# The sine product of the q and k rotations on VectorE instead of GpSimd

## The chip, the cores and the metric

The kernel runs on one core of a Trainium2 chip. The core has five engines with a queue each: TensorE (PE in the profile, its weight loads PEld), VectorE (DVE), ScalarE (ACT), GpSimd (POOL) and SyncE (SP). Each engine works through a queue of its own in the program's order, and semaphores hold an instruction until what it needs is there. The metric is the device time of one execution in microseconds (us); less is better.

## The reference, cut to what matters

Two networks follow one another, of two layers each, on 512 tokens of width 1024. One mixing layer of the first network is a differential attention of 8 heads; both mixing layers of the second contain, among other attentions, a dilated attention with three branches of four heads. In these, queries and keys are rotated by their position before the scores:

```python
def rotate_half(t):
    half = t.shape[-1] // 2
    return jnp.concatenate([-t[..., half:], t[..., :half]], axis=-1)

def diff_attention_mixer(x, w_qkv, ...):
    ...
    q = (q * cos + rotate_half(q) * sin) * (DIFF_HEAD_DIM ** -0.5)
    k = k * cos + rotate_half(k) * sin
    ...
    scores = jnp.einsum('bhmqd,bhmkd->bhmqk', q[:, :, :, s0:s1], k[:, :, :, :s1], ...)
    p = jax.nn.softmax(jnp.where(mask, scores, NEG_INF), axis=-1)
    attn = p[:, :, 0] - lam * p[:, :, 1]

def _mixing(x, w_in, ...):
    ...
    q = br(_rope(flat(q), pos))
    k = br(_rope(flat(k), pos))
    o_dil = _dilated_attention([q[:, :, i] for i in range(N_BR)], ...)
```

## The kernel before, in words

All products run in an exact split form: a float32 matrix is split into a high part (`split`, L217, a copy on ScalarE) and a low part (L218, a subtraction on VectorE), and `mm3` (L266 to L268) adds three matmuls. Weights arrive in 1024-column halves and are split the same way; they appear as `wpart` and `wmore`.

A rotation (`rope2`, L1185) works on one 128x512 tile of q or k that TensorE has just finished in PSUM: one column group of two heads, or of one head with two maps. Four 32-row pieces are moved into a scratch tile `sh`, two by ScalarE (L1191) and two by VectorE (L1192). The scratch is multiplied by the sines (L1193), the PSUM tile by the cosines (L1194, VectorE), the two are added (L1195, VectorE), and the sum is split into its parts (L217, L218; tiles `dr` in the differential attention, `qd` in the mixing layers of the second network). There are 40 rotations: 16 in the differential attention (4 at its start, 12 in its heads), 12 in each of the two later mixing layers.

In the differential attention the heads run as one pipeline (`diff_head`, `pipelined`). Of each of four query tiles i = 0..3 of a head: scores on TensorE (L872, with the mask L874), two maxima (L876, VectorE), two exponentials with their sums (L878, ScalarE), a reciprocal, a small product and the difference of the two maps (L884, L885, L886, VectorE), transposes on TensorE (L1232) copied out by ScalarE (L1234), and the product with the values (L894). The q and k columns of the next heads (`diff_qk`, 16 steps of three matmuls a head, two rotations a head) are woven in between, and so are the splits of the weights that a later head needs (`done`, `pump`). TensorE's order is the program's own (`manual_schedule`); the queues of VectorE, ScalarE and GpSimd are ordered by a scheduler from the dependences, so a change of one instruction can move others. A half of a weight part may be overwritten only when TensorE has finished the step that still reads it.

Of a head's two rotations, the one that falls near the scores of tile 2 is called the early one below, the one near tile 3 the late one.

Of the kernel before, what the change touches and what calls it, by code (L numbers as in the profile page):

```python
# [129 lines left out]
class _Net:  # L130
# [1054 lines left out]
    def rope2(self, ps, parts, classes, scale=1.0):  # L1185


        nc = self.nc
        sh, t = self.grab(), self.grab()
        for o in (0, 64):  # L1190
            nc.scalar.activation(sh[o:o + 32], ps[o + 32:o + 64], AF.Copy, scale=scale)  # L1191
            nc.vector.tensor_scalar(sh[o + 32:o + 64], ps[o:o + 32], scale, None, op0=ALU.mult)  # L1192
        nc.gpsimd.tensor_mul(sh, sh, self.c("sin"))  # L1193
        nc.vector.scalar_tensor_tensor(t, ps, scale, self.c("cos"), op0=ALU.mult, op1=ALU.mult)  # L1194
        nc.vector.tensor_add(t, t, sh)  # L1195
        if classes:
            parts = [x.rearrange("p (r j) -> p j r", r=4) for x in parts]
            self.split(*parts, t.rearrange("p (j r) -> p j r", r=4))
        else:
            self.split(*parts, t)  # L1200
        self.drop(sh, t)
# [1110 lines left out]
```

## Time and profile before

| | |
|---|---|
| median of 3 runs | 2736.17 us (2734.69 to 2741.09) |
| profiled execution | 2736.06 us, span 2734.3 us |
| TensorE matmul busy | 2610.4 us (95%) |
| VectorE busy | 1663.5 us (61%) |
| ScalarE busy | 1313.9 us (48%) |
| GpSimd busy | 452.2 us (17%) |

The span is the time from the first to the last instruction of the profiled execution; what is left to its own time lies outside. Shares are means over stages with different limits. A busy TensorE is a TensorE with a matmul in flight, and a few matmul records are missing from the trace.

### The profile page before, as it was taken

The numbers are of one execution on the slowest core, as the hardware profiler recorded it, in microseconds if no ns is written. First come the engines' busy times: TensorE is split into PE (matmuls) and PEld (weight loads), VectorE is DVE, ScalarE is ACT, GpSimd is POOL, SyncE is SP. The second block draws the span as 40 slices with busy tenths as digits, with TensorE's granted clock in tenths as the row PEclk, the third lists the DMA queues.
The fourth block names the chain that finished last, engine by engine and source line by source line (L and its number), as shares of the span: only waits on it lengthen the run. The fifth ranks groups of instructions, "written<-read, shape, count | busy, mean of one in ns | idle before, by whom it ended". The sixth has DMA issues, their size and how long they took to land. (4 is left out here: it accounts for less than half of the span.)

```text
span 2734.3 us, 41301 instructions
## 1 busy us (share of the span) xinstructions
PE 2610.4 (95%) x14504; PEld 2194.2 (80%) x14508; DVE 1663.5 (61%) x2633; ACT 1313.9 (48%) x2074; POOL 452.2 (17%) x430
## 2 busy tenths in 40 slices
PE   8999999999999999999999979999899999899996
PEld 6768888887668888898887768888788877788884
DVE  7786333376866333366445586669774455847887
ACT  5644222255644222245464436558654554246784
POOL 2324000010114000002021121211120211212112
PEclk9999999999999999999999989999999999899998
DMA  6114232313104323224202059979532030479995
GB/s 228 52 47 170 93 101 93 108 64 108 62 32 143 104 87 107 96 90 155 87 28 108 19 190 290 307 216 364 179 129 98 32 118 19 152 242 296 346 356 183
DMA packets 94490, 389.23 MB, mean 142 GB/s; under 512 B 14880, under 2 KB 16672, under 8 KB 77984
## 3 DMA queue, kind: packets, MB, share of 16 engines
q1 hardware_dynamic: 76592, 329.14, 34.1%
q0 software_dynamic: 14624, 51.52, 6.9%
q10 hardware_dynamic: 3024, 5.56, 0.6%
q8 instruction: 118, 1.93, 0.3%
q14 instruction: 132, 1.08, 0.1%
HBM read 351.31 MB, written 34.87 MB: 141 GB/s over the span
## 5 line engine op out<-in xcount | busy, mean ns | idle before, releaser
L218 DVE TENSOR_TENSOR wpart<-raw,wpart 128x1024 fp32r<-128x1024 f32 (+3 forms) x393 | 532.5, 1384 | 289.8 <-ACT wpart L217 280.4
L217 ACT ACTIVATE wpart<-raw 128x1024 fp32r<-128x1024 f32 (+3 forms) x393 | 446.4, 1169 | 364.7 <-PE mm L267 182.4
L266 PE MATMUL mm<-xT,wpart 128*128 128x512 f32 (+1 forms) x1136 | 438.2, 386 | 22.0 <-ACT wpart L217 9.0
L267 PE MATMUL mm<-xT,wpart 128*128 128x512 f32 (+1 forms) x1136 | 425.4, 375 | 1.9 <-DVE xT L218 1.9
L268 PE MATMUL mm<-xT,wpart 128*128 128x512 f32 (+1 forms) x1136 | 425.5, 375 | 0.5 <-DVE wpart L218 0.5
L266 PEld LDWEIGHTS mm<-xT,wpart 128*128 128x128 f32 x1136 | 216.6, 191 | 59.8 <-ACT wpart L217 9.0
L268 PEld LDWEIGHTS mm<-xT,wpart 128*128 128x128 f32 x1136 | 215.9, 190 | 39.4 <-DVE wpart L218 1.0
L267 PEld LDWEIGHTS mm<-xT,wpart 128*128 128x128 f32 x1136 | 216.4, 190 | 37.1 <-DVE xT L218 2.9
L266 PE MATMUL mm<-wpart,xT 128*128 128x256 f32 (+2 forms) x672 | 241.1, 359 | 0.0
L268 PE MATMUL mm<-wpart,xT 128*128 128x256 f32 (+2 forms) x672 | 227.0, 339 | 0.4 <-DVE xT L218 0.3
L267 PE MATMUL mm<-wpart,xT 128*128 128x256 f32 (+2 forms) x672 | 226.1, 336 | 0.0
L352 POOL TENSOR_TENSOR sm<-sm,mhalf 128x4 f32<-128x4 f32 (+2 forms) x66 | 61.0, 925 | 978.0 <-DVE sm L365 728.1
L267 PE MATMUL mm<-wpart,gT 128*128 128x256 f32 (+1 forms) x544 | 186.9, 344 | 2.2 <-DVE wpart L218 2.2
L268 PE MATMUL mm<-wpart,gT 128*128 128x256 f32 (+1 forms) x544 | 184.1, 338 | 0.0
L266 PE MATMUL mm<-wpart,gT 128*128 128x256 f32 (+1 forms) x544 | 183.9, 338 | 0.0
L571 DVE TENSOR_TENSOR silu<-silu,mm 128x512 f32<-128x512 f32 x44 | 30.2, 686 | 194.5 <-PE mm L268 194.5
L266 PEld LDWEIGHTS mm<-wpart,xT 128*128 128x128 f32 x672 | 127.8, 190 | 18.0 <-issue 5.2
L218 DVE TENSOR_TENSOR xT<-raw,xT 128x1024 fp32r<-128x1024 f32 x108 | 130.0, 1221 | 15.9 <-ACT xT L217 15.3
L268 PEld LDWEIGHTS mm<-wpart,xT 128*128 128x128 f32 x672 | 127.6, 190 | 14.1 <-DVE xT L939 1.0
L267 PEld LDWEIGHTS mm<-wpart,xT 128*128 128x128 f32 x672 | 128.0, 190 | 9.6 <-issue 1.2
L266 PE MATMUL mm<-xT,hT 128*128 128x512 f32 x272 | 112.9, 415 | 5.7 <-DVE rt L2125 4.5
L267 PEld LDWEIGHTS mm<-wpart,gT 128*128 128x128 f32 x544 | 104.2, 191 | 17.0 <-DVE wpart L218 4.3
(590 smaller groups left out, 5632.8 us busy)
## 6 DMA issues: line engine op xcount, KB each, us to landing
raw<-in_w_dram SPq DMA_DIRECT2D x324, 512.0 KB, 7.4
raw<-in_gu_dram SPq DMA_DIRECT2D x40, 1024.0 KB, 4.7
raw<-in_w_in_dram SPq DMA_DIRECT2D x30, 1024.0 KB, 4.8
raw<-in_down_dram SPq DMA_DIRECT2D x16, 1024.0 KB, 5.1
raw<-in_o_qk_dram SPq DMA_DIRECT2D x8, 1024.0 KB, 4.7
raw<-in_w_out_dram SPq DMA_DIRECT2D x8, 1024.0 KB, 5.2
raw<-in_e_in_dram SPq DMA_DIRECT2D x7, 1024.0 KB, 7.3
raw<-in_down_dram SPq DMA_DIRECT2D x8, 768.0 KB, 4.3
```

The source lines that it names most:

```text
L217: ins = self.nc.scalar.activation(hi, x, AF.Copy)
L218: self.last_lo = (eng or self.nc.vector).tensor_sub(lo, x, hi)
L266: mm(out, lhsT=ls[0], rhs=rs[0], start=start, stop=False)
L267: mm(out, lhsT=ls[0], rhs=rs[1], start=False, stop=False)
L268: mm(out, lhsT=ls[1], rhs=rs[0], start=False, stop=stop)
L352: self.last_rsqrt = self.nc.gpsimd.tensor_tensor(v, v, self.half[:, :n], op=ALU.pow)
L571: nc.vector.tensor_mul(s, s, ps[2 * j + 1])
```

## The change

One line: the multiplication of the scratch tile by the sines is issued on VectorE instead of GpSimd. Operands, sizes and results are the same.

```diff
@@ rope2
         for o in (0, 64):
             nc.scalar.activation(sh[o:o + 32], ps[o + 32:o + 64], AF.Copy, scale=scale)
             nc.vector.tensor_scalar(sh[o + 32:o + 64], ps[o:o + 32], scale, None, op0=ALU.mult)
-        nc.gpsimd.tensor_mul(sh, sh, self.c("sin"))
+        nc.vector.tensor_mul(sh, sh, self.c("sin"))
         nc.vector.scalar_tensor_tensor(t, ps, scale, self.c("cos"), op0=ALU.mult, op1=ALU.mult)
         nc.vector.tensor_add(t, t, sh)
```

The orders of TensorE and SyncE are the same before and after. On VectorE 40 products come in, and some neighbours move with them.

VectorE at the late rotation of a head of the differential attention (`df` are its float tiles, `sm` small columns, `s` the scores in PSUM, `wpart` weight halves); five heads have this piece:

```order
+L1193 TENSOR_TENSOR df_3822<-df_3822,cf 128x512
 L876 TENSOR_REDUCE sm_4689<-s_4688 128x1
 L1195 TENSOR_TENSOR df_3823<-df_3823,df_3822 128x512
+L218 TENSOR_TENSOR wpart_88<-raw_92,wpart_87 128x1024
+L218 TENSOR_TENSOR dr_3826<-df_3823,dr_3825 128x512
 L884 RECIPROCAL sm_4538<-sm_4537 128x2
+L876 TENSOR_REDUCE sm_4730<-s_4728 128x1
 L885 SCALAR_TENSOR_TENSOR sm_4702<-sm_4537,lneg,sm_4538 128x1
+L876 TENSOR_REDUCE sm_4730<-s_4729 128x1
 L886 SCALAR_TENSOR_TENSOR df_3813<-df_3818,sm_4702,df_3813 128x512
-L218 TENSOR_TENSOR dr_3826<-df_3823,dr_3825 128x512
-L876 TENSOR_REDUCE sm_4730<-s_4728 128x1
```

The product stands ahead of the second maximum, and the two low parts and the next tile's two maxima, which stood behind the difference L886, now stand ahead of it.

ScalarE at the same place (the two L878 of tile 3 are the exponentials of the two maps):

```order
 L878 ACTIVATE df_3813,sm_4537<-s_4687,sm_4689 128x512
 L1234 ACTIVATE df_3824<-t_4713 128x384
+L217 ACTIVATE wpart_87<-raw_92 128x1024
+L217 ACTIVATE dr_3825<-df_3823 128x512
 L878 ACTIVATE df_3818,sm_4537<-s_4688,sm_4689 128x512
-L217 ACTIVATE dr_3825<-df_3823 128x512
-L217 ACTIVATE wpart_87<-raw_92 128x1024
```

The two high parts stood behind the second exponential and now stand ahead of it.

VectorE at the early rotation of a head:

```order
 L1192 TENSOR_SCALAR df_3823<-mm_4517 32x512
 L1194 SCALAR_TENSOR_TENSOR df_3813<-mm_4517,cf 128x512
+L1193 TENSOR_TENSOR df_3823<-df_3823,cf 128x512
 L884 RECIPROCAL sm_4538<-sm_4537 128x2
 L903 TENSOR_REDUCE sm_4629<-df_3814 128x4
```

Here the product is put in and nothing else moves.

## Rows read from the trace of the kernel before

**Rows 1.** The page: busy time, share of the span, instructions.
```profile
PE 2610.4 (95%) x14504; PEld 2194.2 (80%) x14508; DVE 1663.5 (61%) x2633; ACT 1313.9 (48%) x2074; POOL 452.2 (17%) x430
```

**Rows 2.** What TensorE waited for, 585 to 780 us: us, times, longest.
```profile
PE t L1232 <- DVE df L886: 7.2, 16, 0.9
PE t L923 <- DVE xT L939: 3.0, 1, 3.0
```

**Rows 3.** One head's stretch: busy of PE, PEld, DVE, ACT, POOL; clock; DMA.
```profile
719.60:739.50 19.90, 18.72 (x110) 13.69 (x111) 17.30 (x39) 12.33 (x30) 3.58 (x3) 1.00 0.17 54
```

**Rows 4.** Line L1193: durations in ns, and who waited for it.
```profile
L1193 POOL TENSOR_TENSOR df<-df,cf x16: 1272/1286/1807, 594.7 to 766.6; 128x512 f32<-128x512 f32 x16
...
  DVE mx L1195: 7.1, 10
```

**Rows 5.** Line L1195: durations in ns.
```profile
L1195 DVE TENSOR_TENSOR df<-df,df x16: 677/693/695, 596.0 to 767.9; 128x512 f32<-128x512 f32 x16
```

**Rows 6.** Timeline of VectorE at a late rotation: start, us, instruction.
```profile
675.00 0.69 DVE L1194 SCALAR_TENSOR_TENSOR df<-mm,cf 128x512 f32<-128x512 f32 x1
675.61 0.68 DVE L876 TENSOR_REDUCE sm<-s 128x1 f32<-128x512 f32 x1
676.43 0.69 DVE L1195 TENSOR_TENSOR df<-df,df 128x512 f32<-128x512 f32 x1
677.14 0.17 DVE L884 RECIPROCAL sm<-sm 128x2 f32<-128x2 f32 x1
...
677.60 0.75 DVE L886 SCALAR_TENSOR_TENSOR df<-df,sm,df 128x512 f32<-128x512 f32 x1
678.27 0.68 DVE L218 TENSOR_TENSOR dr<-df,dr 128x512 fp32r<-128x512 f32 x1
678.87 0.48 DVE L876 TENSOR_REDUCE sm<-s 128x1 f32<-128x128 f32 x2
679.27 1.21 DVE L218 TENSOR_TENSOR wpart<-raw,wpart 128x1024 fp32r<-128x1024 f32 x1
```

**Rows 7.** Timeline of ScalarE at the same place.
```profile
676.33 0.69 ACT L878 ACTIVATE df<-s,sm 128x512 f32<-128x512 f32 x1 [0.82 <-DVE sm L876]
...
677.16 0.63 ACT L217 ACTIVATE dr<-df 128x512 fp32r<-128x512 f32 x1
677.70 1.04 ACT L217 ACTIVATE wpart<-raw 128x1024 fp32r<-128x1024 f32 x1
```

**Rows 8.** Timeline of TensorE at these places, with idle time and releaser.
```profile
668.87 0.41 PE L1232 MATMUL t<-cf,df 128*128 128x128 f32 x2 [0.56 <-DVE df L886]
...
675.53 0.40 PE L267 MATMUL mm<-xT,wpart 128*128 128x512 f32 x1
...
678.49 0.63 PE L1232 MATMUL t<-cf,df 128*128 128x128 f32 x4 [0.89 <-DVE df L886]
...
759.32 0.63 PE L1232 MATMUL t<-cf,df 128*128 128x128 f32 x4 [0.20 <-DVE df L886]
```

**Rows 9.** Timeline of VectorE at an early rotation.
```profile
665.54 0.69 DVE L1194 SCALAR_TENSOR_TENSOR df<-mm,cf 128x512 f32<-128x512 f32 x1
...
666.22 0.67 DVE L903 TENSOR_REDUCE sm<-df 128x4 f32<-128x512 f32 x1
666.97 0.69 DVE L1195 TENSOR_TENSOR df<-df,df 128x512 f32<-128x512 f32 x1
```

**Rows 10.** TensorE's longest wait in the first of the two later mixing layers.
```profile
1264.61 0.47 PE L266 MATMUL mm<-xT,wpart 128*128 128x512 f32 x1 [2.57 <-DVE mx L1194]
```

**Rows 11.** Windows just behind two long waits (columns as in rows 3).
```profile
1264.60:1269.00 4.40, 4.39 (x12) 3.50 (x13) 2.44 (x3) 1.83 (x3) 0.56 (x1) 0.61 0.52 216
...
767.40:774.00 6.60, 6.07 (x22) 5.03 (x24) 4.87 (x9) 1.80 (x3) 0.47 (x1) 0.50 0.13 45
```

**Rows 12.** VectorE in the second network's first layer, during and without L1193.
```profile
1227.82 1.89 DVE L218 TENSOR_TENSOR wpart<-raw,wpart 128x1024 fp32r<-128x1024 f32 x1
...
1239.35 1.21 DVE L218 TENSOR_TENSOR wpart<-raw,wpart 128x1024 fp32r<-128x1024 f32 x1
```

## The prediction

> **What bounds the kernel now.** The page comes first: TensorE is busy 95% of the span, VectorE 61% [rows 1], so only what makes TensorE wait, or stops a wait, can change the time. The list of waits, taken for the three stretches that hold rotations, says where that is. In the differential attention (585 to 780 us) TensorE waits 16 times for L886, the difference of the two maps, before the transposes L1232, 7.2 us in all, and once for 3.0 us for L939 [rows 2]. L886 is VectorE work, so there VectorE's queue sets the pace though no mean shows it. The window of one head says the same: of 19.9 us VectorE is busy 17.30 and TensorE 18.72 [rows 3]. In the two later mixing layers TensorE has one long wait each, 2.57 us for L1194 [rows 10]; L1194 is the cosine product, which stands ahead of the sine product in most rotations.
>
> Then the timelines of VectorE, ScalarE and TensorE, around one late and one early rotation of a head. At the late one L886 starts at 677.60 [rows 6] and the transposes of tile 3 at 678.49, after a wait that is recorded as 0.89; in the head at 759.32 it is 0.20 [rows 8]. Either way it is above zero: TensorE is already waiting for L886, so each microsecond by which L886 comes later is paid in full. At the early one the transposes of tile 1 start at 668.87 after 0.56 of waiting for L886 [rows 8].
>
> **The change, part by part.** *The product itself.* On GpSimd it takes 1286 ns [rows 4]. VectorE has a tensor-tensor instruction of the same shape and type, L1195, at 693 ns [rows 5], and independent neighbours start about 0.61 apart (675.00 to 675.61 [rows 6]). So 40 products put 40 x 0.61 = 24 us into VectorE's queue. GpSimd is left with little at these places and nobody waits for what it has left.
>
> *The early rotations of the heads, six, and the first late one.* Nothing else moves there. The product puts 0.61 ahead of L1195 and L886. VectorE gains a little back where L1195 had to wait for GpSimd: L1195 starts at 666.97, 0.75 behind L903, and could start 0.61 behind it [rows 9], so 0.14 goes. L886 comes 0.47 later, and TensorE waits there now: 7 x 0.5 = 3.5 us.
>
> *The five other late rotations.* Here the order moves. I put the new order of VectorE together from durations of rows 6: L1194 at 675.00; product 675.61; second maximum 676.22; L1195 676.83; then the low part of a weight half at 677.44, which takes 1.21; the low part `dr` at 678.65; 0.60 later (678.27 to 678.87) L884 at 679.25. Before, L886 came 0.46 behind L884 (677.14 to 677.60); now the next tile's two maxima lie in between, 0.40 (678.87 to 679.27). L886 starts at 680.11 instead of 677.60, which is 2.5 us later: 0.6 for the product and 1.9 for work that used to run while TensorE was busy with the next tile. ScalarE does not hold it up further: the high part of the weight half can start when TensorE leaves the step that reads it (675.53 + 0.40 [rows 8]), takes 1.04, then `dr` behind L1195's end (677.52) takes 0.63, then the second exponential 0.69 [rows 7], done at 678.84, before 679.25. So TensorE's wait before the transposes of tile 3 becomes about 2.7 us, 5 x 2.5 = 12.5 us. The moved work is gone from behind L886, but that gives nothing back: TensorE's next wait for L886 is some 11 us later (668.87 and a head's 20 us, against 678.49 [rows 3, 8]), and VectorE gets there from TensorE's own next scores, which are late by as much.
>
> *The clock.* Behind a wait of 2.57 us [rows 10] the granted clock is 0.61 in the mean over 4.4 us, that is partly 1.2 instead of 2.4 GHz, which loses 0.39 x 4.4 = 1.7 us [rows 11]. The five new waits are about as long. Lower end: none is followed by a fall, 0 us. Upper end: all five, 8.5 us. The nearest row is a wait that was followed by one; but two such waits, one in each mixing layer, make no rule; I take 3.5 of 5, 6.0 us.
>
> *The start of the differential attention* (four rotations). TensorE runs without a wait there; the later `gain` and split work on VectorE is covered by the value products on TensorE. Nothing; 4 x 0.61 = 2.4 us if that cover were gone.
>
> *The mixing layers* (24 rotations). Upper bound: four products in a row at the start of each, passed on whole, 2 x 2.4 = 4.9 us. Lower bound: L1195 waited 7.1 us for GpSimd at `mx` tiles [rows 4]; all of it back would be -7.1. A second thing comes back there: a weight subtraction that ran beside L1193 took 1.89 where the same takes 1.21 alone [rows 12], 0.68 less for VectorE. But the long waits are for L1194 [rows 10], ahead of the product, and a chain in which GpSimd's 1.3 becomes 0.61 + 0.69 on a queue in order is hardly shorter. I take 0.
>
> Sum: 3.5 + 12.5 + 6.0 = 22.0 us on the profiled execution of 2736.06 us, 2758 us. That execution lies at the median of the runs shown (2736.17), so no correction is needed.
>
> **The rivals.** *Light.* The moved splits cost nothing, because something else (an operand that comes late) holds L886 anyway or the next wait shrinks by what this one grows. Then only the products count: 12 x 0.5 = 6 us, no wait long enough for the clock, 2742 us; with half of the moved work 2747. For it: the total work of a head on VectorE rises by only 1.2 us to 18.5 of about 20 [rows 3]. Against it: L886 stands behind that work in the queue.
>
> *Not slower.* The product is faster where it now runs, and the chain of a rotation is what counts. The long wait for L1194 in each mixing layer [rows 10] ends a chain that has earlier rotations upstream. If the 0.7 that VectorE waits for GpSimd per rotation (7.1 us in 10 [rows 4]) is taken out of it, the wait falls to 1.9, the clock stays up, and each layer gains 0.7 + 1.7 = 2.4 us: -4.8, 2731 us, if at the same time the heads' waits do not grow. The point that decides is whether L886 comes later than TensorE's arrival at the transposes: rows 8 say that it does already. The Trainium skill speaks for this side: the page GPSIMD Engine Reference, section Engine selection, sends elementwise work with two inputs to VectorE and calls GpSimd about twice as slow. The trace agrees on the ratio, 1286 to 693 ns [rows 4, 5]. By that rule alone, all 40 rotations on the path, the estimate would be 40 x 0.59 = 24 us less, 2712 us; the trace shows no wait of TensorE for the product.
>
> *Heavy.* The clock falls behind all five waits and stays down as long as behind the 3.0 us wait [rows 2], where it was 0.50 over 6.6 us [rows 11], 3.3 us lost each: 16.0 + 5 x 3.3 = 32.5, 2768 us. Against it: the wait of 2.57 cost half of that.
>
> **How the numbers follow.** Forecast (2750 to 2766): 0.62. Light (2741 to 2750): 0.15. Not slower (2728 to 2741): 0.12. Heavy (2766 to 2778): 0.11. The predicted time is the forecast's, 2758. The range leaves out the third case and the upper part of the last: 2742 to 2770. A measurement of this kernel can tell some 0.2%, 5.5 us. Above 2741.6 lies the forecast, the heavy case and nearly all of the light one: slower 0.85. Within 0.2%: 0.10, the rest of the light case and most of the third. Faster: 0.05.
>
> **What would show it.** In the profile after, L1193 on VectorE near 0.69 us; TensorE's wait for L886 in 585 to 780 us up from 7.2 to some 23 us, with five single waits of 2.5 to 2.8 before the transposes of tile 3; those of the early rotations near 1.1; a head's period up from about 20 to about 23 us; some of the long waits followed by a clock of 0.5. Between 1205 and 1340 us (shifted by the loss before) the waits should be as before. I am wrong if the five waits stay below 1 us, if the splits on ScalarE wait for a weight step so that the waits exceed 4 us, or if the mixing layers change by more than 2 us each.

## The result, and the profile after

The changed kernel takes 2761.2 us in the median of 4 runs (2759.3 to 2765.3), the kernel before on the same chip 2735.4: a ratio of 1.0091, 95% interval 1.0077 to 1.0105, 25.8 us slower. The forecast was 2758 in a range of 2742 to 2770. The profiled execution of the changed kernel took 2762.03 us with a span of 2760.2.

First the page of the changed kernel, busy time of each engine, beside [rows 1].

```profile
PE 2621.6 (95%) x14508; PEld 2203.5 (80%) x14508; DVE 1681.1 (61%) x2673; ACT 1315.2 (48%) x2074; POOL 397.3 (14%) x390
```

VectorE has 40 more instructions and 17.6 us more to do, GpSimd 40 fewer and 54.9 us less. On the page nobody is fuller than before: VectorE stays at 61%. So the page does not show where 25.8 us come from; the list of waits of TensorE in the differential attention does, beside [rows 2] (us, times, longest; 585 to 800 us, since all lies later).

```profile
PE t L1232 <- DVE sm L884: 13.1, 5, 3.0
PE t L1232 <- DVE df L886: 7.4, 11, 1.0
PE t L923 <- DVE xT L939: 3.6, 1, 3.6
```

The transposes L1232 waited 7.2 us before and wait 20.5 now, in the same 16 places. Five of the waits are long, and they are now put down to L884, the instruction ahead of L885 and L886 on VectorE. TensorE's timeline shows the single ones, an early one, then late ones, beside [rows 8].

```profile
669.47 0.41 PE L1232 MATMUL t<-cf,df 128*128 128x128 f32 x2 [0.99 <-DVE df L886]
...
681.22 0.63 PE L1232 MATMUL t<-cf,df 128*128 128x128 f32 x4 [3.03 <-DVE sm L884]
...
730.57 0.63 PE L1232 MATMUL t<-cf,df 128*128 128x128 f32 x4 [2.34 <-DVE sm L884]
...
752.99 0.63 PE L1232 MATMUL t<-cf,df 128*128 128x128 f32 x4 [2.33 <-DVE sm L884]
```

The early wait is 0.99 instead of 0.56. The late ones are 3.03 instead of 0.89 at one head and 2.34 instead of 0.20 at another: both 2.14 more. (The 0.69 between the two kinds is there before as well and is real: VectorE takes 4.73 and 4.74 us from L1194 to L886 at the two heads, but between the value products L894 and the transposes TensorE has one step of the woven q and k work, the matmuls L266 to L268, three times at 730 and twice at 681. One step more, 3 x 0.23 us, fills that much of the wait.) VectorE's timeline at the place of [rows 6] shows what came between.

```profile
675.60 0.69 DVE L1194 SCALAR_TENSOR_TENSOR df<-mm,cf 128x512 f32<-128x512 f32 x1
676.21 0.68 DVE L1193 TENSOR_TENSOR df<-df,cf 128x512 f32<-128x512 f32 x1
676.81 0.68 DVE L876 TENSOR_REDUCE sm<-s 128x1 f32<-128x512 f32 x1
677.41 0.68 DVE L1195 TENSOR_TENSOR df<-df,df 128x512 f32<-128x512 f32 x1
678.01 1.22 DVE L218 TENSOR_TENSOR wpart<-raw,wpart 128x1024 fp32r<-128x1024 f32 x1
679.14 0.68 DVE L218 TENSOR_TENSOR dr<-df,dr 128x512 fp32r<-128x512 f32 x1
679.75 0.16 DVE L884 RECIPROCAL sm<-sm 128x2 f32<-128x2 f32 x1
...
680.01 0.21 DVE L885 SCALAR_TENSOR_TENSOR sm<-sm,lneg,sm 128x1 f32<-128x1 f32 x1
680.13 0.28 DVE L876 TENSOR_REDUCE sm<-s 128x1 f32<-128x128 f32 x1
680.34 0.74 DVE L886 SCALAR_TENSOR_TENSOR df<-df,sm,df 128x512 f32<-128x512 f32 x1
```

From L1194 to L886 it was 2.60 us (675.00 to 677.60 [rows 6]) and is 4.74. There is no idle time in the chain: the product, the weight half and the split of the rotation stand ahead of L886 one behind the other. ScalarE's second exponential at the same place, with the read-out of its sum, is done at 679.42, 0.33 before L884 starts:

```profile
678.66 0.67 ACT L878 ACTIVATE df<-s,sm 128x512 f32<-128x512 f32 x1
...
679.23 0.19 ACT L878 ACTIVATION_READ_ACCUMULATOR df<-s,sm 128x1 f32 x1
```

The clock behind two of the long waits and behind the wait for L939 (us, busy time of PE, PEld, DVE, ACT, POOL; granted clock; DMA share, GB/s), beside [rows 11]:

```profile
681.20:685.60 4.40, 4.38 (x18) 3.81 (x19) 0.57 (x2) 0.60 (x1) 0.00 (x0) 0.61 0.00 0
...
730.57:735.00 4.43, 4.43 (x29) 3.59 (x30) 1.50 (x5) 2.49 (x4) 0.00 (x0) 1.00 0.00 0
...
787.80:794.40 6.60, 6.60 (x33) 5.55 (x34) 5.27 (x13) 1.86 (x3) 1.01 (x1) 0.75 0.00 1
```

Behind four of the five waits the mean clock is 0.61 to 0.63 over some 4.4 us, partly 1.2 instead of 2.4 GHz; behind the wait at 730 it stays at 1.00. In the same 4.4 us TensorE gets through 18 instructions instead of 29. Behind the wait for L939 the clock is 0.75 over 6.6 us, where it was 0.50.

In the first later mixing layer the long wait is as in [rows 10]:

```profile
1282.86 0.77 PE L266 MATMUL mm<-xT,wpart 128*128 128x512 f32 x1 [2.51 <-DVE mx L1194]
```

It also serves as a mark: this matmul starts at 1264.61 before [rows 10], so the changed kernel is 18.3 us late here. All of the forecast's 22.0 was to lie ahead of this mark. The other 7.6 us of the 25.9 by which the spans differ arise behind it.

### The profile page after: what moved, and what is told of

Read it like the earlier page. It is cut to its first block, busy times and chain, and to the rows that moved or that the text cites. A ratio compares the mean times of both kernels' runs of the same rounds, so it can differ in the third digit from the quotient of the medians.

```text
span 2760.2 us, 41225 instructions
## 1 busy us (share of the span) xinstructions
PE 2621.6 (95%) x14508; PEld 2203.5 (80%) x14508; DVE 1681.1 (61%) x2673; ACT 1315.2 (48%) x2074; POOL 397.3 (14%) x390
## 5 line engine op out<-in xcount | busy, mean ns | idle before, releaser
L266 PE MATMUL mm<-xT,wpart 128*128 128x512 f32 (+1 forms) x1136 | 440.7, 388 | 21.2 <-ACT wpart L217 8.4
L268 PE MATMUL mm<-xT,wpart 128*128 128x512 f32 (+1 forms) x1136 | 427.6, 377 | 0.5 <-DVE wpart L218 0.5
L266 PEld LDWEIGHTS mm<-xT,wpart 128*128 128x128 f32 x1136 | 217.6, 192 | 59.0 <-ACT wpart L217 8.4
L268 PEld LDWEIGHTS mm<-xT,wpart 128*128 128x128 f32 x1136 | 217.3, 191 | 39.7 <-DVE wpart L218 1.0
L266 PE MATMUL mm<-wpart,xT 128*128 128x256 f32 (+2 forms) x672 | 241.3, 359 | 0.0
L268 PE MATMUL mm<-wpart,xT 128*128 128x256 f32 (+2 forms) x672 | 227.2, 339 | 0.4 <-DVE xT L218 0.3
L268 PE MATMUL mm<-wpart,gT 128*128 128x256 f32 (+1 forms) x544 | 184.4, 339 | 0.0
L266 PE MATMUL mm<-wpart,gT 128*128 128x256 f32 (+1 forms) x544 | 184.3, 339 | 0.0
L266 PEld LDWEIGHTS mm<-wpart,xT 128*128 128x128 f32 x672 | 128.0, 191 | 17.9 <-issue 5.3
L268 PEld LDWEIGHTS mm<-wpart,xT 128*128 128x128 f32 x672 | 127.5, 190 | 14.0 <-DVE xT L218 1.2
L266 PE MATMUL mm<-xT,hT 128*128 128x512 f32 x272 | 114.0, 419 | 7.8 <-DVE rt L2125 4.4
L267 PEld LDWEIGHTS mm<-wpart,gT 128*128 128x128 f32 x544 | 104.4, 192 | 17.5 <-DVE wpart L218 5.1
```

The source lines that it names most:

```text
L266: mm(out, lhsT=ls[0], rhs=rs[0], start=start, stop=False)
L267: mm(out, lhsT=ls[0], rhs=rs[1], start=False, stop=False)
L268: mm(out, lhsT=ls[1], rhs=rs[0], start=False, stop=stop)
```

## The experiments

Three marks order all runs: the start of L266 behind its wait for L1194 in the first and in the second later mixing layer, and the end of the span, each as the difference to the kernel before (1264.61, 2023.44, 2734.3), from the profiled execution; then the median of the runs against the runs of the kernel before on the same chip, and the ratio with its interval.

| run | layer 1 | layer 2 | span | median, us | ratio |
|---|---|---|---|---|---|
| changed | +18.3 | +20.1 | +25.9 | +25.8 | 1.0091 [1.0077, 1.0105] |
| e10, changed again | +18.5 | +18.5 | +18.7 | +24.8 | 1.0084 [1.0070, 1.0098] |
| e1, differential attention | +18.9 | +20.9 | +20.9 | +21.1 | 1.0074 [1.0059, 1.0089] |
| e2, mixing layers | -1.2 | -1.6 | +1.0 | -0.8 | 0.9993 [0.9984, 1.0003] |
| e3, late rotations | +17.6 | +17.0 | +17.1 | +17.5 | 1.0060 [1.0047, 1.0073] |
| e4, early rotations | +1.1 | +3.2 | +2.8 | +4.6 | 1.0016 [1.0007, 1.0026] |
| e5, order of before | +4.1 | +6.1 | +3.4 | +9.5 | 1.0029 [1.0018, 1.0040] |
| e7, GpSimd, sum behind | -4.8 | -2.4 | -0.2 | -2.3 | 0.9987 [0.9978, 0.9997] |
| e9, all behind | +0.8 | -0.1 | +2.5 | +2.0 | 1.0004 [0.9994, 1.0014] |
| e11, split ahead | +8.0 | +7.8 | +4.3 | +10.5 | 1.0041 [1.0027, 1.0055] |
| e12, shift alone | +21.3 | +24.3 | +24.7 | +26.6 | 1.0104 [1.0089, 1.0119] |

The first column holds the heads, where the edits are, and what lies ahead of them and between them and the mark. It gives 18.3, 18.5 and 18.9 for three executions with the same edit in the heads, but that is closer than the parts are: e10 starts its heads 2.5 us early, loses more in them and gets less back behind them. From the start of L1194 in the heads' first rotation (654.43 before) to the transposes L923 behind the wait for L939 (767.93 before), the heads alone lose 20.3 us in the changed kernel, 21.5 in e10, 20.2 in e1, 18.2 in e3, 2.7 in e4, 6.4 in e5, 8.6 in e11 and 1.7 in e9; they gain 4.7 in e7; in e2 (0.1 gained) and e12 (0.0), whose heads are those of before, nothing changes. What lies behind the second mark scatters by more than some of the effects (from -3.5 in e11 to +5.8 in the changed kernel, +0.2 in the same kernel again); so what an edit does is read in the first column and in the heads alone, and the median is given beside them.

**Which rotations lose (e1 to e4).** A parameter picks the engine of the product:

```diff
-    def rope2(self, ps, parts, classes, scale=1.0):
+    def rope2(self, ps, parts, classes, scale=1.0, product=None):
...
-        nc.vector.tensor_mul(sh, sh, self.c("sin"))
+        (product or nc.gpsimd).tensor_mul(sh, sh, self.c("sin"))
```

In e1 the call in `rope_new` passes VectorE, in e2 the one in the mixing layers; in e3 only where `j == 0 and h > 2`, the five late rotations in which the order moves; in e4 only where `j == 1`, the six early ones.

Expected of e1: 

> The product on VectorE only in the 16 rotations of the differential attention, on GpSimd in the 24 of the mixing layers. Theory (the loss is made in the heads): nearly all of the change's 25.8 us stays, 20 to 26 us over before, with the waits for L886 in the heads as in the changed kernel. Rival (the mixing layers carry a part): 18 us or less, and the run with the product on VectorE only in the mixing layers has the rest.

Expected of e2: 

> The product on VectorE only in the 24 rotations of the two mixing layers, on GpSimd in the differential attention. Theory: those rotations lie behind work that TensorE does not wait for, so the time is that of before, within 2 us either way. Rival (mixing layers lose, as their stretch seemed to by 1.5 to 2 us and the stretch behind 2500 us by 5.6): 2 to 7 us over before. Rival (not slower, the product is the faster one where the chain of a rotation counts): up to 5 us under before.

Expected of e3: 

> The product on VectorE only in the five late rotations of the heads in which the order moves, 5 of 40. Theory (the splits and maxima that come ahead of L886 are the loss): five waits of TensorE of 2.3, 5 x 2.1 = 10.7 us, and about 4 falls of the clock at 1.7, 13 to 18 us over before. Rival (VectorE's load alone, each product paying its own 0.6 wherever it stands): 5 x 0.6 = 3 us.

Expected of e4: 

> The product on VectorE only in the six early rotations of the heads, where the order of the next instructions stays. Theory: each L886 comes 0.4 to 0.5 later and no wait is long enough for the clock, 2.6 us over before (2 to 4). Rival (VectorE's load alone): 6 x 0.6 = 3.6, not to be told apart here, but then it equals the run with the late rotations alone. Rival (all rotations of the heads cost alike): 6/11 of what the changed kernel lost there, 10 us.

Measured: e1 has the whole loss of the heads (+18.9), e2 none: 24 of the 40 products moved without a trace in the time. Of the loss at the first mark five products make 17.6 and six make 1.1. So it is not the load alone, since each of the eleven products is the same addition to the same queue. TensorE's waits in e3, 585 to 800 us:

```profile
PE t L1232 <- DVE sm L884: 13.1, 5, 3.0
PE t L1232 <- DVE df L886: 4.6, 11, 0.6
```

The five long waits are those of the changed kernel to 0.1 us, with the other eleven as short as before. Here all five are followed by a lower clock. In e4 the single waits are those of the changed kernel: 0.42 to 0.49 more at five early rotations, and at the sixth the wait for L939 is 0.60 longer (2.97 to 3.57), 2.8 in all, which is what the heads alone lose. Its 1.1 at the first mark is less, since here too the clock comes back earlier behind the wait for L939 (0.77 over 6.6 us instead of 0.50); e12 below has the same without a rotation touched. e4's median, 4.6 over before, is outside the expected 2 to 4; the difference arises behind the first mark, where it goes from +1.1 to +3.2.

**The order alone (e5, e11).** e5 has all products on VectorE and takes the moved work back behind L886; e11 is the opposite, GpSimd's product with a part of the moved work forced ahead of L886. In e5 the split of a late rotation is kept back until the scores of the tile have been written out, and it and the weight halves are then queued behind the tile's second exponential (`e`) and its L886 (`d`):

```diff
+            self.drop(pm[1]); self.last = e, d; self.marks = (e, d) if i == NT - 1 and h < 6 else self.marks
...
+    def queue(self, marks, work):
+        a, b = [self.tc.issue_after(m.ins) if m else nullcontext() for m in marks]
+        with a, b:
+            while work: work.pop(0)()
...
+        self.queue(self.last, self.tail)
...
+            self.queue(self.marks, [self.pending.pop(0)])
...
-            self.split(*parts, t)
+            self.tail.append(lambda: self.split(*parts, t)) if late else self.split(*parts, t)
```

In e11, made from the kernel before:

```diff
+            split_first = self.tc.issue_after(self.last_lo.ins) if i == NT - 1 and 0 < h < 6 else nullcontext()
...
-            nc.vector.reciprocal(rd, r.den[:, :, i])
+            with split_first: nc.vector.reciprocal(rd, r.den[:, :, i])
```

Expected of e5: 

> All 40 products on VectorE, but in the five late rotations the weight half, the split and the next maxima stand behind L886 again, as before; the product stays ahead of it. Theory (the loss of the late rotations is the moved order): waits of TensorE there of about 0.8 to 1.2 us instead of 2.3, no fall of the clock; 12 x 0.5 = 6 us over before (4 to 9). Rival (VectorE has simply no room for the products): the changed kernel's 20 to 26 us over before.

Expected of e11: 

> The kernel before, product on GpSimd, with one half of the moved order forced: in the five late rotations the split of the rotation and the next two maxima stand ahead of L886, the weight half stays behind it. Theory (what stands ahead of L886 is paid, whoever put it there): L886 later by 0.6 and 0.2 to 0.4, TensorE's waits at tile 3 longer by 0.8 to 1.0 each, no fall of the clock: 4 to 5 us over before. Rival (the moved work costs only together with the product): within 1 us of before.

VectorE at the same late rotation in e5:

```profile
675.39 0.69 DVE L1194 SCALAR_TENSOR_TENSOR df<-mm,cf 128x512 f32<-128x512 f32 x1
676.00 0.68 DVE L1193 TENSOR_TENSOR df<-df,cf 128x512 f32<-128x512 f32 x1
...
677.20 0.68 DVE L1195 TENSOR_TENSOR df<-df,df 128x512 f32<-128x512 f32 x1
678.12 0.17 DVE L884 RECIPROCAL sm<-sm 128x2 f32<-128x2 f32 x1 [0.25 <-ACT df L878]
678.33 0.22 DVE L885 SCALAR_TENSOR_TENSOR sm<-sm,lneg,sm 128x1 f32<-128x1 f32 x1
678.58 0.75 DVE L886 SCALAR_TENSOR_TENSOR df<-df,sm,df 128x512 f32<-128x512 f32 x1
679.25 0.69 DVE L218 TENSOR_TENSOR dr<-df,dr 128x512 fp32r<-128x512 f32 x1
```

L1194 to L886 is 3.19 us: the product alone costs 0.59. It is paid by way of ScalarE: the product stands ahead of the second maximum, and VectorE waits 0.25 for the exponential L878 that needs this maximum. TensorE's waits at tile 3 there are 1.49 and 0.80 in place of 0.89 and 0.20, so 0.60 more, and the clock behind them stays up:

```profile
679.48:683.90 4.42, 4.42 (x29) 3.58 (x30) 3.02 (x8) 2.59 (x8) 0.00 (x0) 1.00 0.00 0
```

The loss at the first mark falls from 18.3 to 4.1, and that of the heads alone from 20.3 to 6.4, with the same 40 products on the same engine. In the median e5 is 9.5 over before (7.9 by the ratio), above the expected 4 to 9 by the median and inside it by the ratio; its profiled execution is the fastest of its seven, and what the others lose beyond the heads no trace shows.

In e11 no product is on VectorE, and 8.0 are lost at the first mark, twice what was expected. VectorE at the late rotation:

```profile
675.65 0.69 DVE L1194 SCALAR_TENSOR_TENSOR df<-mm,cf 128x512 f32<-128x512 f32 x1
...
677.08 0.69 DVE L1195 TENSOR_TENSOR df<-df,df 128x512 f32<-128x512 f32 x1
678.47 0.69 DVE L218 TENSOR_TENSOR dr<-df,dr 128x512 fp32r<-128x512 f32 x1 [0.70 <-ACT dr L217]
679.08 0.16 DVE L884 RECIPROCAL sm<-sm 128x2 f32<-128x2 f32 x1
...
679.67 0.74 DVE L886 SCALAR_TENSOR_TENSOR df<-df,sm,df 128x512 f32<-128x512 f32 x1
```

The expectation had forgotten that the split's low part needs its high part from ScalarE: VectorE stands still for 0.70 before it. L1194 to L886 is 679.67 - 675.65 = 4.02, which is 1.42 more than before, and so are the waits (2.31 and 1.55 instead of 0.89 and 0.20). That is 5 x 1.4 = 7.0; the rest goes with one fall of the clock, behind one of the five. So work moved ahead of L886 is paid without any change of engine. In the changed kernel the weight half lies in the time for which VectorE stands still here: from L1195 to the low part `dr` it is 1.73 us there (677.41 to 679.14) and 1.39 here, so the weight half itself adds only 0.34, and the split with its wait for ScalarE makes the rest.

**Everything behind L886 (e7, e9).** With the same queue, in eleven rotations of the heads (six late, five early), e7 keeps the product on GpSimd and puts L1195 and the split behind L886; e9 has the product on VectorE and puts product, L1195 and split behind it (the line below is e9's; in e7 the addition alone stands in place of `*rest`):

```diff
-            self.split(*parts, t)
+            self.tail.extend([*rest, lambda: self.split(*parts, t)]) if late else self.split(*parts, t)
```

Expected of e7: 

> The product on GpSimd as before, but in eleven rotations of the heads the addition L1195 and the split are queued behind L886, the weight halves too. Theory (what stands ahead of L886 in VectorE's queue is paid by TensorE): the waits for L886, 7.2 us in all before, fall to 2 us or less, and the time to 3 to 6 us under before. Rival (L886 is held by an operand, not by the queue): no change, within 2 us.

Expected of e9: 

> All 40 products on VectorE, and in eleven rotations of the heads the product, the addition and the split are queued behind L886. Theory (the place in the queue decides, not the load): waits for L886 as in the kernel with the addition behind it, the time that of before or up to 5 us under it. Rival (VectorE's load): 11 x 0.6 = 6.6 us over the kernel with the addition behind and the product on GpSimd, or more.

e7: the waits for L886 up to 780 us fall from 7.2 to

```profile
PE t L1232 <- DVE df L886: 2.5, 5, 0.9
```

and at the first mark e7 is 4.8 us ahead of before. Only half of it is left at the second mark and 2.3 in the median, less than the expected 3 to 6 and hardly to be told from no change, though the interval ends just under 1. The waits at the early rotations and at tile 2 are gone; the five that are left (0.88, 0.88, 0.32, 0.20 and 0.19) are all at tile 3, about as long as before, and at the place of [rows 6] VectorE stands still before L884 although L1195 no longer lies ahead of it:

```profile
676.46 0.17 DVE L884 RECIPROCAL sm<-sm 128x2 f32<-128x2 f32 x1 [0.84 <-ACT df L878]
```

So the theory holds at the early rotations and at tile 2. The late ones fit the rival: an operand, ScalarE's second exponential, is as late as the queue there, and taking L1195 out of the way of L886 gives nothing. e9 is the harder test of my theory, and it holds only in half. The waits at tile 1 (early) and tile 3 (late) are gone or at most 0.27, but one at tile 2 has come:

```profile
674.32 0.52 PE L1232 MATMUL t<-cf,df 128*128 128x128 f32 x3 [1.58 <-DVE df L886]
```

It was 0.36 at this place before. VectorE shows why:

```profile
671.33 0.68 DVE L218 TENSOR_TENSOR dr<-df,dr 128x512 fp32r<-128x512 f32 x1
671.92 0.16 DVE L884 RECIPROCAL sm<-sm 128x2 f32<-128x2 f32 x1
672.12 0.68 DVE L1192 TENSOR_SCALAR df<-mm 32x512 f32<-32x512 f32 x1
672.83 0.22 DVE L885 SCALAR_TENSOR_TENSOR sm<-sm,lneg,sm 128x1 f32<-128x1 f32 x1
672.97 0.68 DVE L876 TENSOR_REDUCE sm<-s 128x1 f32<-128x512 f32 x1
673.57 0.61 DVE L886 SCALAR_TENSOR_TENSOR df<-df,sm,df 128x384 f32<-128x384 f32 x1
```

What was put behind one L886 now stands, together with the first sine half and a maximum of the next tile, ahead of the next L886. The waits for L886 sum to 8.6 us up to 780, against 2.5 in e7 and 7.2 before: five waits of 1.5 to 1.8. So e9 loses 5.6 us to e7 at the first mark and 6.4 in the heads alone, close to the 6.6 of the rival, and lands at the time of before. Place decides how a product is paid, but between one L886 and the next VectorE has little room left.

**What is lost behind the heads (e10, e12).** e10 is the changed kernel again. e12 is the kernel before with 86 matmuls that nothing reads ahead of the value products of the differential attention:

```diff
-                self.weave(self.diff_values(v))
+                [nc.tensor.matmul(p, lhsT=xT[0][:, 0, :P], rhs=xT[0][:, 0], start=True, stop=True) for p in (self.ps("mm"), self.ps("mm")) for _ in range(43)]; self.weave(self.diff_values(v))
```

Expected of e10: 

> The changed kernel again, word for word, beside the others on one chip, for the 5.6 us that its profile has behind 2500 us and that no part run shows: with differential attention alone the change cost 21.0, with the mixing layers alone -0.8. Theory (the tail is spread of the executions): 20 to 23 us over before. Rival (the two parts together cost more than apart): 25 to 27.

Expected of e12: 

> The kernel before with 86 matmuls of 128x512 that nothing reads at the start of the differential attention, about 18.5 us of TensorE at full clock, so that all behind it lies as late as in the changed kernel, without a rotation touched. Theory (a shift alone moves the clock's falls behind 1590 us and the traffic of the last expert stage): 20 to 25 us over before. Rival (the 5 to 7 us behind the heads belong to the change): 18 to 19 us, the shift alone.

e10's median is 24.8 over before, between the two expectations, while its profiled execution, the fastest of the five by 4.6 us, ends 18.7 over it: what was lost at the first mark and nothing more. So two executions of one program differ by 7.2 us, all of it behind the first mark. Whether the two parts of the change cost more together than apart stays open: the intervals of the changed kernel, e10 and e1 overlap. e12's 86 matmuls, put at 18.5 us, keep TensorE busy for

```profile
L791 PE MATMUL mm<-xT 128*128 128x512 f32 x86 | 19.7, 390 | 0.0
```

(busy us, mean ns, idle before), and the time goes up by 26.6 in the median and 24.7 in the span: 6.9 and 5.0 us more than these matmuls, with the median above the expected 20 to 25 and the span inside it, with no rotation touched and the waits for L886 as before (7.1 us in 16). Its windows show two of the places, behind the wait for L939 and in a stretch of the next stage, the latter beside the same stretch in the kernel before:

```profile
788.20:794.80 6.60, 6.60 (x34) 5.41 (x33) 5.30 (x12) 2.13 (x5) 0.00 (x0) 0.74 0.04 15
870.00:876.60 6.60, 6.26 (x41) 6.24 (x41) 5.41 (x4) 2.79 (x4) 0.00 (x0) 0.74 0.52 217
```

```profile
850.00:856.60 6.60, 6.26 (x52) 6.13 (x52) 5.63 (x5) 2.90 (x5) 0.22 (x1) 1.00 0.58 221
```

The first is 0.50 in [rows 11] and gives 1.6 us back; the second is at 1.00 in the kernel before and costs 1.7. A third place where executions part is the start of the last expert stage, where the DMA engines are full. The same 100 us of program, before, changed, e10 and e12, each window put behind by the run's lateness at 2500 us:

```profile
2500.00:2600.00 100.00, 97.45 (x590) 85.88 (x589) 88.33 (x96) 78.61 (x100) 17.97 (x11) 1.00 1.01 344
```

```profile
2520.00:2620.00 100.00, 94.45 (x556) 81.77 (x556) 84.89 (x93) 76.51 (x97) 17.46 (x11) 1.00 1.00 331
```

```profile
2519.00:2619.00 100.00, 97.58 (x591) 85.80 (x591) 88.42 (x97) 78.79 (x101) 17.36 (x11) 1.00 1.00 346
```

```profile
2524.00:2624.00 100.00, 96.43 (x560) 83.27 (x559) 85.23 (x93) 77.37 (x98) 16.93 (x11) 0.98 1.00 334
```

At the same full share of the DMA engines, 344 to 346 GB/s go with 590 instructions of TensorE, 331 to 334 with some 558. The changed kernel has it both ways, in two executions. The other profiled executions lie between, at 339 to 343 GB/s, or above, at 351 (e11), and a late start of this stage does not decide it: e3, 17 us late, has 342. In e12 the lower rate costs nothing in the end (+24.3 at the second mark, +24.7 at the end). Why one execution gets the lower rate stays open.

Nor does a shift by itself always cost. e3 is 17.6 us late at the first mark, 17.1 at the end, and 17.5 in the median of six runs. The step of about 2 us between the first and the second mark comes in runs that are hardly shifted (e4, e7) as in late ones (changed, e1). In most runs it goes with the clock of the next stage: over 80 us (1580.00 to 1660.00 before, moved by the first mark) the mean is 0.87 before and in e2, 0.85 in e3, e9, e11 and e12, and 0.83 in the changed kernel, e1, e4, e5 and e7, but also in e10, which has no such step, and e12 has one at 0.85. So e12 shows that a delay can cost what the changed kernel lost behind the heads; why it does in one run and not in another is not shown.

## Why the prediction held, point by point

**The product ahead of L886** was set at 0.6 a rotation; e5 shows 0.59. At five early rotations the wait grew by 0.41 to 0.49 (0.47 reckoned), at the first late one by 0.53, and the sixth early one lengthened the wait for L939 by 0.66 (2.97 to 3.63), a place that the prediction did not name. Seven of them: 3.4 instead of 3.5 us.

**The moved work** is the cause, as the prediction had it, and its term, the product included, was a sixth too large: the five waits grew by 2.06 to 2.14, 10.6 us instead of 12.5. The order came as put together from [rows 6]. Two sizes were off. The two maxima were charged 0.40; L885 starts some 0.2 us behind L884 also where nothing lies between (678.12 to 678.33 in e5), one maximum lies in that gap, and L884 to L886 grew from 0.46 (677.14 to 677.60 [rows 6]) to 0.59 only, 0.13. And the weight half holds the queue for 1.13 (678.01 to 679.14), not for its full 1.21. That ScalarE would not hold it up further was right for the changed kernel (0.33 us to spare), but only because the weight half stands where VectorE would otherwise wait for ScalarE: the prediction gave it 1.21 of the 2.5, and against e11 it adds 0.34.

**The clock**: 3.5 falls of five were taken, there were four, and five in e10 and e3. By the heads' times a fall costs a little less than 1.7: of the 20.3 us that the heads alone lost, the waits explain 20.5 - 7.2 = 13.3 and the longer wait for L939 0.7. That leaves 6.3 for four falls, 1.6 each, where the prediction had 6.0 for 3.5. What it did not have is the earlier return of the clock behind the wait for L939, which gave back 1.6 ((0.75 - 0.50) x 6.6); with heads that started 0.4 early this makes the 18.3 of the first mark. In e10, the same program, the clock there is 0.54, and nearly nothing comes back. None of the five waits of e5 (0.60 longer than before), one of the five of e11 (1.4 longer) and 18 of the 20 here, in e10, e1 and e3 (about 2.1 longer) was followed by a fall.

**The mixing layers and the start of the differential attention** were put at nothing. e2 agrees: -0.8 us, ratio 0.9993. The page GPSIMD Engine Reference of the Trainium skill, section Engine selection, by which elementwise work with two inputs belongs on VectorE, is right about the speed (0.68 against 1.29 us) and says nothing about the time: 24 products moved by that rule gained nothing, and twelve of the other 16 cost.

**The sum** came out three us low, and that it is so close is in part luck: two errors cancel. At the first mark 18.3 are lost instead of 22.0. What the prediction did not have is a term for what happens behind the heads, where all starts 18 us later; this was taken as free. The profiled execution lost 7.6 us there, e10's 0.2, and e3, as late, nothing; e12 lost 5.0 to 6.9 beyond its delay without a rotation touched. With the heads' loss alone the right forecast would have been 2754, inside the range.

**The rivals.** Light fell: in the changed kernel the queue holds L884 until 679.75, and the operand from ScalarE is there at 679.42. It had a point that e7 shows: at tile 3 that operand holds L886 once the queue is clear. But the moved work holds it longer. Heavy's clock was half right, five falls can happen, but each ends as behind the 2.57 of [rows 10], none lasts as behind the 3.0. Not slower fell at its own point: L886 was late already.

## What to carry to other kernels

A faster instruction on a fuller engine is judged by what stands behind it in that engine's queue. Ask which instruction another engine is already waiting for; what the move puts ahead of that one is paid, 0.4 to 0.6 us here for the product itself, and some two and a half times as much (1.55) for the work that shifted along with it. Print the new order before costing the edit, and look at what else changed place. When an effect is under one per cent, read it at a mark just behind the edit: the rest of the program moved by up to 7 us here between executions of one kernel. A plain delay of the same size shows whether a late start alone can make such a difference; more than one execution is needed to see whether it does.

## What the runs showed of the hardware

A delay of TensorE need not be paid just once. 86 matmuls that nothing reads kept it busy for 19.7 us and cost 26.6, while e3, 17.6 us late at the first mark, took 17.5 us longer in the median. The granted clock has a part in it: it comes back at another moment behind the same wait (0.50 over 6.6 us before, 0.74 in e12; 0.75 and 0.54 in two executions of the changed kernel) and falls at places where it did not fall before (0.74 instead of 1.00 in e12's next stage). The DMA engines at a full share moved 331 to 351 GB/s in the same stretch of the program; what that costs is not shown.

The collision in [rows 12], 1.89 us for a weight subtraction beside GpSimd's product and 1.21 without, is gone in the changed kernel, where the product is on VectorE at 1246.53 and the subtraction behind it takes 1.22:

```profile
1247.13 1.22 DVE L218 TENSOR_TENSOR wpart<-raw,wpart 128x1024 fp32r<-128x1024 f32 x1
```

The page Perfetto Trace Analysis of the Trainium skill, section Optimizing Scalar/DVE Operations, warns that work passed between these two engines might not help because they share a read port; the trace agrees, with 0.68 us more for that subtraction. Its end gave nothing back in e2, since TensorE does not wait for it there.
